# The last pair's row norm ahead of the other pair's transposes at the ends of MLPs and output projections

## The chip, the cores and the metric

The kernel runs on one core of one Trainium2 chip. The metric is the device time of one execution in microseconds (us). Before the change three timed runs gave a median of 3179.25 us (3178.51 to 3179.38). The engines are named as in the profile: PE (TensorE, matmuls and transposes), PEld (its weight loads), DVE (VectorE), ACT (ScalarE), POOL (GpSimd), SP (the queue that issues most DMAs).

## The reference

A forward pass over 512 tokens of 1024 features in fp32, batch 1. The first block has two layers, each a mixer and an MLP with a norm before and after each:

```
for layer in range(DEPTH):
    hn = _rms_norm(x, norm_mix_pre[layer])
    mix = sparse attention + short convolution   # layer 0, ends in @ w_out
          or latent attention                    # layer 1, ends in @ w_o
    x = x + _rms_norm(mix, norm_mix_post[layer])
    hn = _rms_norm(x, norm_ffn_pre[layer])
    x = x + _rms_norm(square(relu(hn @ w1)) @ w2, norm_ffn_post[layer])
```

The second block takes this x with a context of 256 tokens and runs a differential attention and a neighbourhood attention, each on `rms_norm(x) * (1 + scale) + shift` and added back with a gate.

So at the end of each mixer and each MLP of the first block stands the same piece of work: a projection to 1024 columns, an RMS norm of each token's row of the result (the post norm), its addition to x, and an RMS norm of the new row of x (the next norm), whose output feeds the next projection.

## The kernel before

**Products.** An fp32 product is made from three matmuls on halves (`mm3`, L587 to L589): high by high, then the two mixed products of high and low. Every operand therefore exists twice, as hh and hl for activations and as w_hi and w_lo for weights.

**Weights.** `WeightStream` brings weights in units of 128 x 1024 (or 128 x 768). Its `split` takes one unit: ACT casts it to w_hi (L276), POOL subtracts to get w_lo in pieces of two feature blocks (L280), or DVE does this in one instruction where `tick(nc.vector)` is called; then the load of a later unit is issued on SP. `tick` splits the next unit if fewer than `ring` = 4 are ahead of what `release` has given back. So the place of a `tick` in the program sets where cast and subtraction stand in their engines' queues.

**Rows.** The 512 tokens are four tiles of 128 rows, in two pairs. `rows_gemm` (L615) computes such a projection in four column blocks c = 0 to 3 of 256 columns. Blocks 0 and 1 run over all tiles; blocks 2 and 3 go pair by pair, so that pair 0 is complete early. After each tile `evac` squares the result on ACT with a row sum (op_sq), and DVE writes M = result times gain (L1092; in the MLP L1203 and L1206). After a pair's last block comes `tail`: a tick, `post` (L606: sum of squares po_ss, reciprocal root by ACT's rs_y and DVE's rs_a and po_r, then two updates of X, L613), a tick with DVE, and `nx.stat`, the next norm of that pair: squares of X on ACT, reciprocal root, and the scaled rows nf_y on DVE and ACT (L328, L330).

**Transposes.** `Next.flush` turns nf_y into the next stage's operand: for every two feature blocks PE transposes into PSUM (tp, L338), ACT writes hh (L413) and DVE writes hl (L347). Where the next stage has a shift (after MLP 1), DVE writes nf_f (L350), ACT hh, and POOL hl (L416). A pair has eight feature blocks, four such parts. By `PARTS` two parts of pair 0 follow the first tile of pair 1 in block 3 and two follow the second, in front of pair 1's `tail`. Pair 1's own parts are issued by the next stage when it comes to its second half (`need`).

Each engine works off its own queue in program order; a semaphore wait at the head of a queue holds everything behind it. The next stage begins with pair 0's tokens: for an MLP, `first` multiplies four weight units with the 256 columns of pair 0, feature block k = 0 to 7 with three matmuls each, then transposes pair 1 and does the same for its columns.

The places are the ends of the output projection of layer 0 (o0, near 346 us), MLP 0 (near 735), the output projection of layer 1 (o1, near 1010) and MLP 1 (near 1394).

Of the kernel before, what the change touches and what calls it, by code (L numbers as in the profile page):

```python
# [32 lines left out]
def plan():  # L33
# [5 lines left out]
    def mlp(l):  # L39
# [6 lines left out]
        return r  # L46

    p += mlp(0)
    p += [(f"dq:{h}", 2, 384) for h in range(4)]
    p += [(f"dkv:{h}", 3 if h < 2 else 2, 288) for h in range(3)]  # L50
# [6 lines left out]
    p += [(f"v2:7:{h}", 4, 256) for h in range(2)]  # L57
    p += [(f"o1:{c}:{h}", 4, 256) for c in range(4) for h in range(2)]
    p += mlp(1)
    for L in (2, 3):  # L60
        def two(n, g):
# [181 lines left out]
PARTS = ((0, 0), (0, 0), (0, 2), (0, 2))  # L243


class WeightStream:
# [38 lines left out]
    def tick(s, eng=None):  # L285
        if s.halved < min(len(s.units), s.done + s.ring):
            s.split(eng)
# [15 lines left out]
class Next:  # L303
# [55 lines left out]
    def flush(s, n=4):  # L359

        parts = s.pend[0][1]
        for _ in range(min(n, len(parts))):
            parts.pop(0)()
        if not parts:
            s.pend.pop(0)
# [15 lines left out]
class Net:  # L381
# [230 lines left out]
        for j in range(2):  # L612
            nc.vector.scalar_tensor_tensor(s.X[i + j], M[i + j], r[:, j:j + 1], s.X[i + j], OP.mult, OP.add)  # L613

    def rows_gemm(s, keys, lhs, evac, tail, npair, flush, wide_first=False, mid=None, k_first=False):  # L615

        nc = s.nc

        def part(ps, i, u, ks, first, last):
            wh, wl = u  # L620
            t = slice(i * 128, (i + 1) * 128)
            for b, k in enumerate(ks):
                ah, al = lhs(k)
                s.mm3(ps, ah[:, t], al[:, t], wh[:, b], wl[:, b], first and b == 0, last and b == len(ks) - 1)

        def tile(i, c, us, parts=(0, 0)):
            ps = s.mm.tile([128, 512], F32, name="mm")[:, :256]
            for j, (u, ks) in enumerate(us):
                part(ps, i, u, ks, j == 0, j == len(us) - 1)
                if j == 0 and parts[0]:  # L630
                    flush(parts[0])
            s.W.tick()
            evac(i, c, ps)
            if parts[1]:
                flush(parts[1])

        def get(c):
            return [(s.W.get(k), ks) for k, ks in keys(c)]

        def pair(i, c, us, free, between):  # L640

            ps = [s.mm.tile([128, 512], F32, name="mm")[:, :256] for _ in range(2)]
            for j, (u, ks) in enumerate(us):
                for t in range(2):
                    part(ps[t], i + t, u, ks, j == 0, j == len(us) - 1)
                    if free and t:
                        s.W.release(s.W.i - len(us) + 1 + j)
                    s.W.tick()
                    if j == len(us) - 1:
                        evac(i + t, c, ps[t])  # L650
                if j == 0:
                    between()

        n = 2 * npair
        for c in range(2):
            s.W.release()
            us = get(c)
            if c == 0 and wide_first:
                for i0 in range(0, n, 4):
                    ps = [s.mm.tile([128, 512], F32, name="mm")[:, :256] for _ in range(i0, min(n, i0 + 4))]  # L660
                    if k_first:
                        us = [([x[:, b:b + 1] for x in u], [k]) for u, ks in us for b, k in enumerate(ks)]
                    for j, (u, ks) in enumerate(us):
                        for i, q in enumerate(ps):
                            part(q, i0 + i, u, ks, j == 0, j == len(us) - 1)
                    for i, q in enumerate(ps):
                        s.W.tick()
                        evac(i0 + i, c, q)
            elif c == 0:
                for i in range(n):  # L670
                    if mid:
                        mid(i)
                    tile(i, c, us)
            else:
                for i in range(0, n, 2):
                    if mid:
                        mid(4 + i)
                    pair(i, c, us, i == n - 2, lambda: mid and mid(5 + i))
        s.W.release()
        base = s.W.i  # L680
        us = {2: get(2)}
        for p in range(npair):
            for c in (2, 3):
                if c not in us:
                    us[c] = get(c)
                for j in range(2):
                    tile(2 * p + j, c, us[c], PARTS[2 * c + j - 4] if p else (0, 0))
                if p == npair - 1:
                    s.W.release(base + len(us[2]) * (c - 1))
            tail(2 * p, s.W.tick if p == npair - 1 else lambda e=None: None)  # L690
# [390 lines left out]
    def out_proj(s, name, order, lhs, M, ssp, rowt, sqp, make, gain, part=None, late=None):  # L1081

        nc = s.nc

        def evac(i, c, ps):
            cs = slice(c * 256, (c + 1) * 256)
            if part and c == 0:
                nc.vector.tensor_tensor(part[i], part[i], ps, OP.add)
                ps = part[i]
            sq = sqp.tile([128, 256], F32, name="op_sq")  # L1090
            s.act(sq, ps, AF.Square, acc=ssp[:, i, c:c + 1])
            nc.vector.tensor_tensor(M[i][:, cs], ps, rowt[:, cs], OP.mult)  # L1092
            if late and (c, i) == (1, 0):
                late()

        nx = make()

        def tail(i, tick):
            tick()
            s.post(M, ssp, i)  # L1100
            tick(nc.vector)
            nx.stat(s.X[i:i + 2], i, s.p(gain, 0, 8))

        keys = lambda c: [(f"{name}:{c}:{h}", range(4 * h, 4 * h + 4)) for h in (order if c or not part else order[1:])]
        s.rows_gemm(keys, lhs, evac, tail, 2, lambda n: nx.flush(n), wide_first=True, k_first=part is not None)
        return nx

    def mlp(s, l, nx):
        nc, io = s.nc, s.io
        hh, hl = nx.hi, nx.lo  # L1110
        with s.phase():
# [7 lines left out]
            M = [mp.tile([128, D], F32, name=f"M{i}") for i in range(4)]  # L1119
            ssp = mp.tile([128, 4, 4], F32, name="ssp")  # L1120
            g = {}
# [76 lines left out]
            nx = s.after_mlp(l)  # L1198
# [7 lines left out]
                nc.vector.tensor_tensor(M[i][:, cs], t, rowt[:, cs], OP.mult)  # L1206

            def tail(i, tick):
                tick()
                s.post(M, ssp, i)  # L1210
                tick(nc.vector)
                nx.stat(s.X[i:i + 2], i, *nx.gains)
                if l == 0 and i == 0:
                    nx.keep()
                s.keep_x(0 if l else 2, i)

            keys = lambda c: [(f"w2.{l}:3:{c}:{h}", range(4 * h, 4 * h + 4)) for h in range(2)]
            s.rows_gemm(keys, lambda k: g[3, k], evac, tail, 2, lambda n: nx.flush(n), mid=getattr(nx, "mid", None))
        return nx

    def mlp1(s, nx):
# [1169 lines left out]
```

## Time and profile before

| | us |
|---|---|
| median of three timed runs | 3179.25 |
| profiled execution, its own time | 3187.93 |
| its span | 3186.2 |
| PE busy | 3063.2 (96%) |
| DVE busy | 1908.9 (60%) |
| POOL busy | 1742.4 (55%) |
| ACT busy | 1613.7 (51%) |

The profiled execution is one run with the hardware profiler on. In a timeline each row gives start, duration, engine, line, operation, output<-inputs and count; a bracket at the end is the idle time before it on its engine and who ended that. A PE row's duration overlaps the next one's, as matmuls are pipelined. Granted clock 1.00 means TensorE at its upper level.

### The profile page before, as it was taken

To read this page: it belongs to the slowest core of one execution; us is meant where nothing else is said; L and a number is where in the kernel's file an instruction comes from. 1 tells how busy PE (TensorE), PEld (TensorE's weight loads), DVE (VectorE), ACT (ScalarE), POOL (GpSimd) and SP (SyncE) were. 2 spreads that over 40 slices of the span, in tenths; PEclk is the share of its full clock that TensorE was granted. 3 is DMA by queue.
4 is the path that set the end of the run, shared out by engine and by line. 5 is a ranking of instruction groups with operands and counts; after the bars stand their busy time and mean duration, and the time that the engine had idled before them with its cause. 6 is when DMAs were issued, how large, how long until landed. Compare 5 with 4: busy or idle time off the path is not lost.

```text
span 3186.2 us, 59888 instructions
## 1 busy us (share of the span) xinstructions
PE 3063.2 (96%) x22868; PEld 2883.9 (91%) x22868; DVE 1908.9 (60%) x4161; ACT 1613.7 (51%) x3811; POOL 1742.4 (55%) x2398
## 2 busy tenths in 40 slices
PE   8999999998999999998999999998999999999989
PEld 7898889887999988898999999998999999999989
DVE  4875423345774333455777777777445777777764
ACT  4544533345775433344655555555325656555652
POOL 5543466664563666666556655563356455555545
PEclk9999999999999999999999999999999999999989
DMA  3122333434233444422222222213333233333234
GB/s 123 60 74 82 104 126 132 147 115 142 92 95 109 137 142 136 133 94 76 69 70 61 75 69 66 67 61 102 116 105 87 74 88 84 90 90 89 86 96 140
DMA packets 104555, 310.89 MB, mean 98 GB/s; under 512 B 19902, under 2 KB 33470, under 8 KB 100684
## 3 DMA queue, kind: packets, MB, share of 16 engines
q1 hardware_dynamic: 94908, 271.60, 26.4%
q0 software_dynamic: 7776, 31.46, 4.3%
q10 hardware_dynamic: 1584, 4.00, 0.4%
q8 instruction: 181, 2.97, 0.4%
q14 instruction: 106, 0.87, 0.1%
HBM read 258.73 MB, written 23.12 MB: 88 GB/s over the span
## 4 chain that ended last, share of the span: by engine, by line
PE 62%; DVE 4%; ACT 3%; DMA 3%; POOL 2%; issue 1%; SPq 0%; DVEq 0%; ACTq 0%; POOLq 0%
PE mm L587 16%; PE mm L589 15%; PE mm L588 15%; PE mm L2165 3%; DMA KL<-KL 2%; PE s L2105 2%; PE tp L2304 2%; PE tp L2152 1%; PE s L2106 1%; POOL w_lo L280 1%; PE mm L2319 1%; PE mm L2314 1%; ACT X L413 1%; PE s L2278 1%; PE tp L1843 1%
## 5 line engine op out<-in xcount | busy, mean ns | idle before, releaser
L280 POOL TENSOR_TENSOR w_lo<-w_raw,w_hi 128x256 fp32r<-128x256 f32 (+2 forms) x1446 | 1145.7, 825 | 816.2 <-ACT w_hi L276 786.3
L587 PE MATMUL mm<-w_hi,hh 128*128 128x256 f32 (+2 forms) x2752 | 803.0, 292 | 11.6 <-ACT w_hi L276 4.4
L588 PE MATMUL mm<-w_lo,hh 128*128 128x256 f32 (+2 forms) x2752 | 784.7, 285 | 5.4 <-POOL w_lo L280 3.9
L589 PE MATMUL mm<-w_hi,hl 128*128 128x256 f32 (+2 forms) x2752 | 783.8, 285 | 1.1 <-POOL hl L416 1.1
L587 PEld LDWEIGHTS mm<-w_hi,hh 128*128 128x128 f32 x2752 | 525.8, 191 | 22.1 <-ACT df_sq L413 8.5
L588 PEld LDWEIGHTS mm<-w_lo,hh 128*128 128x128 f32 x2752 | 526.5, 191 | 14.2 <-POOL w_lo L280 8.9
L589 PEld LDWEIGHTS mm<-w_hi,hl 128*128 128x128 f32 x2752 | 525.0, 191 | 2.5 <-POOL hl L416 1.8
L276 ACT CAST w_hi<-w_raw 128x1024 fp32r<-128x1024 f32 (+2 forms) x371 | 383.0, 1036 | 210.5 <-PE mm L589 171.1
L587 PE MATMUL mm<-hh,w_hi 128*128 128x256 f32 (+1 forms) x1408 | 455.5, 324 | 3.0 <-DVE M L1092 2.9
L588 PE MATMUL mm<-hl,w_hi 128*128 128x256 f32 (+1 forms) x1408 | 449.0, 319 | 0.6
L589 PE MATMUL mm<-hh,w_lo 128*128 128x256 f32 (+1 forms) x1408 | 447.6, 318 | 0.6 <-DVE w_lo L280 0.6
L587 PEld LDWEIGHTS mm<-hh,w_hi 128*128 128x128 f32 x1408 | 266.8, 190 | 30.8 <-issue 5.2
L587 PE MATMUL mm<-w_hi,gh 128*128 128x256 f32 x1024 | 287.8, 281 | 0.0
L589 PE MATMUL mm<-w_hi,gl 128*128 128x256 f32 x1024 | 287.1, 280 | 0.1
L588 PEld LDWEIGHTS mm<-hl,w_hi 128*128 128x128 f32 x1408 | 266.9, 190 | 22.3 <-DVE hl L347 1.7
L588 PE MATMUL mm<-w_lo,gh 128*128 128x256 f32 x1024 | 287.0, 280 | 0.0
L589 PEld LDWEIGHTS mm<-hh,w_lo 128*128 128x128 f32 x1408 | 266.5, 189 | 21.4 <-DVE w_lo L280 1.0
L416 DVE TENSOR_TENSOR gl<-rsq,gh 128x512 fp32r<-128x512 f32 x64 | 46.2, 721 | 268.7 <-ACT gh L413 268.7
L587 PEld LDWEIGHTS mm<-w_hi,gh 128*128 128x128 f32 x1024 | 193.2, 189 | 0.4
L589 PEld LDWEIGHTS mm<-w_hi,gl 128*128 128x128 f32 x1024 | 193.0, 188 | 0.5 <-DVE gl L416 0.5
L588 PEld LDWEIGHTS mm<-w_lo,gh 128*128 128x128 f32 x1024 | 193.0, 188 | 0.3
L1831 POOL TENSOR_TENSOR SZ<-SZ,ge 128x128 f32<-128x128 f32 x154 | 80.3, 523 | 162.2 <-DVE ge L1829 68.9
(385 smaller groups left out, 6948.8 us busy)
## 6 DMA issues: line engine op xcount, KB each, us to landing
w_raw<-in_w SPq DMA_DIRECT2D x352, 512.0 KB, 3.6
modw<-in_mod SPq DMA_DIRECT2D x24, 1024.0 KB, 5.7
KH<-KH POOLq DMA_DIRECT2D x32, 384.0 KB, 3.5
KL<-KL POOLq DMA_DIRECT2D x32, 384.0 KB, 4.9
xs<-X SPq DMA_DIRECT2D x12, 512.0 KB, 3.6
X<-xs SPq DMA_DIRECT2D x12, 512.0 KB, 8.4
yd<-ob SPq DMA_DIRECT2D x16, 384.0 KB, 2.5
w_raw<-in_w SPq DMA_DIRECT2D x8, 552.0 KB, 3.6
```

The costliest lines, as they stand in the source:

```text
L276: nc.scalar.copy(hi[:, :m], raw[:, :m])
L280: (eng or nc.gpsimd).tensor_tensor(lo[:, c], raw[:, c], hi.bitcast(F32)[:, c], OP.subtract)
L413: return s.nc.scalar.activation(out, in_, func, bias=bias, scale=scale, **kw)
L416: (eng or s.nc.vector).tensor_tensor(lo, x, hi.bitcast(F32), OP.subtract)
L587: mm(ps, ah, bh, start=first, stop=False)
L588: mm(ps, ah, bl, start=False, stop=False)
L589: mm(ps, al, bh, start=False, stop=last)
L1831: nc.gpsimd.tensor_tensor(z, z, x, OP.mult)
L1843: nc.tensor.transpose(pt[:, j], rawt[n][:, i, pr * 128:(pr + 1) * 128], s.ident)
L2105: nc.tensor.matmul(o, q, KH[:, h, a:b], start=True, stop=False)
L2165: nc.tensor.matmul(ps, x["w"][:, k], V[g][:, kb, p * 128:(p + 1) * 128], start=k == 0, stop=k == nk - 1)
L2304: nc.tensor.transpose(t[:, k], x["P"][:, k * 128:(k + 1) * 128], s.ident)
```

## The change

`rows_gemm` gets a flag `early_post`, set by `out_proj` and `mlp`. With it, a tick stands ahead of the first tile of the last pair's block 3, and the last tile issues no transposes. `tail` now does `post` first, then (for the last pair) the two parts of transposes that the last tile left, then two ticks, both with POOL, then `nx.stat`.

```
-    def rows_gemm(s, keys, lhs, evac, tail, npair, flush, wide_first=False, mid=None, k_first=False):
+    def rows_gemm(s, keys, lhs, evac, tail, npair, flush, wide_first=False, mid=None, k_first=False, early_post=False):
...
                 for j in range(2):
-                    tile(2 * p + j, c, us[c], PARTS[2 * c + j - 4] if p else (0, 0))
+                    last = p == npair - 1 and c == 3 and early_post
+                    if last and j == 0:
+                        s.W.tick()
+                    tile(2 * p + j, c, us[c], (0, 0) if not p or last and j else PARTS[2 * c + j - 4])
...
         def tail(i, tick):
+            s.post(M, ssp, i)
+            if i:
+                nx.flush(2)
             tick()
-            s.post(M, ssp, i)
-            tick(nc.vector)
+            tick()
             nx.stat(s.X[i:i + 2], i, s.p(gain, 0, 8))
```

The tail of `mlp` is changed in the same way. PE's order and SP's do not change. On DVE at the end of o0, where M_3774 and M_3775 are the last two tiles and X_68 and X_69 their rows, the order before is:

```order
L1092 TENSOR_TENSOR M_3775<-mm,rowt 128x256
L347 SCALAR_TENSOR_TENSOR hl<-tp,par,hh 128x256 x4
L609 TENSOR_REDUCE po_ss<-ssp 128x2
L422 TENSOR_SCALAR rs_v<-po_ss 128x2
L432 TENSOR_TENSOR rs_a<-rs_y 128x2
L433 SCALAR_TENSOR_TENSOR rs_a<-rs_a,rs_v 128x2
L434 SCALAR_TENSOR_TENSOR po_r<-rs_a,rs_y 128x2
L613 SCALAR_TENSOR_TENSOR X_68<-M_3774,po_r,X_68 128x1024
L613 SCALAR_TENSOR_TENSOR X_69<-M_3775,po_r,X_69 128x1024
L280 TENSOR_TENSOR w_lo<-w_raw,w_hi 128x1024
L422 TENSOR_SCALAR rs_v<-nf_ss 128x2
```

and now, at the same place:

```order
L1095 TENSOR_TENSOR M_3775<-mm,rowt 128x256
L609 TENSOR_REDUCE po_ss<-ssp 128x2
L422 TENSOR_SCALAR rs_v<-po_ss 128x2
L432 TENSOR_TENSOR rs_a<-rs_y 128x2
L433 SCALAR_TENSOR_TENSOR rs_a<-rs_a,rs_v 128x2
L434 SCALAR_TENSOR_TENSOR po_r<-rs_a,rs_y 128x2
L613 SCALAR_TENSOR_TENSOR X_68<-M_3774,po_r,X_68 128x1024
L613 SCALAR_TENSOR_TENSOR X_69<-M_3775,po_r,X_69 128x1024
L347 SCALAR_TENSOR_TENSOR hl<-tp,par,hh 128x256 x4
L422 TENSOR_SCALAR rs_v<-nf_ss 128x2
```

The four hl of pair 0 (feature blocks 4 to 7) went from in front of the row norm to behind it, and the w_lo of DVE is gone (POOL has it). On ACT at the same place the order before is:

```order
L276 CAST w_hi<-w_raw 128x1024
L413 ACTIVATE op_sq,ssp<-mm 128x256
L413 ACTIVATE hh<-tp,par 128x256 x4
L276 CAST w_hi<-w_raw 128x1024
L413 ACTIVATE op_sq,ssp<-mm 128x256
L413 ACTIVATE hh<-tp,par 128x256 x4
L276 CAST w_hi<-w_raw 128x1024
L413 ACTIVATE rs_y<-po_ss,eps 128x2
L413 ACTIVATE rs_y<-rs_y 128x2
L276 CAST w_hi<-w_raw 128x1024
L413 ACTIVATE nf_y,nf_ss<-X_68 128x1024
```

and now:

```order
L276 CAST w_hi<-w_raw 128x1024 x2
L413 ACTIVATE op_sq,ssp<-mm 128x256
L413 ACTIVATE hh<-tp,par 128x256 x4
L413 ACTIVATE op_sq,ssp<-mm 128x256
L413 ACTIVATE rs_y<-po_ss,eps 128x2
L413 ACTIVATE rs_y<-rs_y 128x2
L413 ACTIVATE hh<-tp,par 128x256 x4
L276 CAST w_hi<-w_raw 128x1024 x2
L413 ACTIVATE nf_y,nf_ss<-X_68 128x1024
```

The second unit's cast moved ahead of the first hh block; the third and fourth moved behind the second hh block. At MLP 1, where POOL also writes hl, POOL's order before is:

```order
L280 TENSOR_TENSOR w_lo<-w_raw,w_hi 128x256 x28
L416 TENSOR_TENSOR hl<-nf_f,hh 128x256 x4
L280 TENSOR_TENSOR w_lo<-w_raw,w_hi 128x256 x4
L416 TENSOR_TENSOR hl<-nf_f,hh 128x256 x4
L280 TENSOR_TENSOR w_lo<-w_raw,w_hi 128x256 x4
```

and now:

```order
L280 TENSOR_TENSOR w_lo<-w_raw,w_hi 128x256 x32
L416 TENSOR_TENSOR hl<-nf_f,hh 128x256 x8
L280 TENSOR_TENSOR w_lo<-w_raw,w_hi 128x256 x8
```

The four w_lo of the second unit stand ahead of all hl, and eight w_lo (those of the third unit, and of the fourth, which DVE did) behind them.

## Rows read from the trace of the kernel before

**Rows 1.** The page: busy us (share of span) and instructions by engine.
```profile
PE 3063.2 (96%) x22868; PEld 2883.9 (91%) x22868; DVE 1908.9 (60%) x4161; ACT 1613.7 (51%) x3811; POOL 1742.4 (55%) x2398
```

**Rows 2.** Timeline of PE, end of o0: start, us, ..., [idle before <-releaser].
```profile
346.58 0.39 PE L587 MATMUL mm<-hh,w_hi 128*128 128x256 f32 x1 [1.40 <-DVE M L1092]
...
349.45 0.39 PE L588 MATMUL mm<-hl,w_hi 128*128 128x256 f32 x1
...
356.20 0.39 PE L589 MATMUL mm<-hh,w_lo 128*128 128x256 f32 x1 [0.33 <-DVE w_lo L280]
...
358.88 1.48 PE L338 MATMUL tp<-ident,nf_y 128*128 128x128 f32 x12
361.69 0.63 PE L338 MATMUL tp<-ident,nf_y 128*128 128x128 f32 x4 [1.33 <-DVE hl L347]
```

**Rows 3.** Timeline of DVE, end of o0, norm of pair 1.
```profile
346.10 0.42 DVE L1092 TENSOR_TENSOR M<-mm,rowt 128x256 f32<-128x256 f32 x1 [0.82 <-ACT op_sq L413]
346.47 0.48 DVE L347 SCALAR_TENSOR_TENSOR hl<-tp,par,hh 128x256 fp32r<-128x256 f32 x1
...
348.91 0.48 DVE L347 SCALAR_TENSOR_TENSOR hl<-tp,par,hh 128x256 fp32r<-128x256 f32 x1 [0.54 <-ACT hh L413]
349.31 0.15 DVE L609 TENSOR_REDUCE po_ss<-ssp 128x2 f32<-128x8 f32 x1
...
350.69 0.66 DVE L433 SCALAR_TENSOR_TENSOR rs_a<-rs_a,rs_v 128x2 f32<-128x2 f32 x1
...
352.15 2.86 DVE L613 SCALAR_TENSOR_TENSOR X<-M,po_r,X 128x1024 f32<-128x1024 f32 x2
```

**Rows 4.** Timeline of DVE, o0, norm of pair 0.
```profile
333.00 0.15 DVE L609 TENSOR_REDUCE po_ss<-ssp 128x2 f32<-128x8 f32 x1
...
334.34 2.48 DVE L613 SCALAR_TENSOR_TENSOR X<-M,po_r,X 128x1024 f32<-128x1024 f32 x2
```

**Rows 5.** Timeline of POOL, end of o0.
```profile
341.65 2.83 POOL L280 TENSOR_TENSOR w_lo<-w_raw,w_hi 128x256 fp32r<-128x256 f32 x4 [16.85 <-ACT w_hi L276]
```

**Rows 6.** Timeline of ACT, end of o0.
```profile
353.84 1.07 ACT L413 ACTIVATE nf_y<-X 128x1024 f32<-128x1024 f32 x1 [2.66 <-DVE X L613]
```

**Rows 7.** Timeline of DVE, end of o1.
```profile
1015.50 2.85 DVE L613 SCALAR_TENSOR_TENSOR X<-M,po_r,X 128x1024 f32<-128x1024 f32 x2
```

**Rows 8.** Timeline of PE, end of MLP 0.
```profile
737.33 0.44 PE L587 MATMUL mm<-w_hi,hh 128*128 128x384 f32 x1 [0.49 <-ACT w_hi L276]
...
742.98 0.69 PE L588 MATMUL mm<-w_lo,hh 128*128 128x384 f32 x1 [0.78 <-DVE w_lo L280]
745.33 1.27 PE L338 MATMUL tp<-ident,nf_y 128*128 128x128 f32 x4 [0.38 <-DVE nf_y L328]
```

**Rows 9.** Timeline of ACT, end of MLP 0.
```profile
740.89 1.06 ACT L413 ACTIVATE nf_y<-X 128x1024 f32<-128x1024 f32 x1 [2.46 <-DVE X L613]
```

**Rows 10.** Windows of PE: stretch, us, PE busy (x), granted clock, DMA share, GB/s.
```profile
740.00:743.00 3.00, 2.22 (x8) 0.50 0.51 147
743.00:747.00 4.00, 3.62 (x12) 0.53 0.77 262
1390.00:1395.00 5.00, 2.43 (x19) 1.00 0.34 105
1395.00:1399.00 4.00, 4.00 (x19) 0.57 0.20 44
```

**Rows 11.** Timeline of PE, end of MLP 1.
```profile
1394.05 0.39 PE L587 MATMUL mm<-w_hi,hh 128*128 128x256 f32 x1 [2.01 <-ACT w_hi L276]
...
1408.61 0.39 PE L587 MATMUL mm<-w_hi,hh 128*128 128x256 f32 x1 [1.81 <-ACT sq L413]
```

**Rows 12.** Timeline of DVE, end of MLP 1.
```profile
1392.07 0.54 DVE L350 TENSOR_SCALAR nf_f<-tp,ada,adb 128x256 f32<-128x256 f32 x1 [2.52 <-POOL hl L416]
...
1401.94 2.92 DVE L613 SCALAR_TENSOR_TENSOR X<-M,po_r,X 128x1024 f32<-128x1024 f32 x2
```

**Rows 13.** Timeline of ACT, end of MLP 1.
```profile
1403.70 1.06 ACT L413 ACTIVATE nf_y<-X 128x1024 f32<-128x1024 f32 x1 [2.65 <-DVE X L613]
```

More of the change, by code (lines that the diff above doesn't have):

```diff
@@ L1098, in tail @@
         def tail(i, tick):
+            s.post(M, ssp, i)
+            if i:
+                nx.flush(2)
             tick()
-            s.post(M, ssp, i)
-            tick(nc.vector)
+            tick()
             nx.stat(s.X[i:i + 2], i, s.p(gain, 0, 8))
         keys = lambda c: [(f"{name}:{c}:{h}", range(4 * h, 4 * h + 4)) for h in (order if c or not part else order[1:])]
-        s.rows_gemm(keys, lhs, evac, tail, 2, lambda n: nx.flush(n), wide_first=True, k_first=part is not None)
+        s.rows_gemm(keys, lhs, evac, tail, 2, lambda n: nx.flush(n), wide_first=True, k_first=part is not None, early_post=True)
         return nx
@@ L1208, in tail @@
             def tail(i, tick):
+                s.post(M, ssp, i)
+                if i:
+                    nx.flush(2)
                 tick()
-                s.post(M, ssp, i)
-                tick(nc.vector)
+                tick()
                 nx.stat(s.X[i:i + 2], i, *nx.gains)
@@ L1217, in mlp @@
             keys = lambda c: [(f"w2.{l}:3:{c}:{h}", range(4 * h, 4 * h + 4)) for h in range(2)]
-            s.rows_gemm(keys, lambda k: g[3, k], evac, tail, 2, lambda n: nx.flush(n), mid=getattr(nx, "mid", None))
+            s.rows_gemm(keys, lambda k: g[3, k], evac, tail, 2, lambda n: nx.flush(n), mid=getattr(nx, "mid", None), early_post=True)
         return nx
```

## The prediction, as it was made before the result was known

> **What bounds the kernel now.** I read the busy times of the page first: TensorE (PE) is busy for 96% of the span, the next engine, DVE, for 60% [rows 1]. So a change pays only where PE stands still, and costs wherever it makes PE stand. Then I read the PE timeline at the four places that the diff touches, looking for brackets (idle time and who ended it), and at each bracket the timeline of the releaser. The reader is to see there which of three streams PE waits for at the end of a stage: the weights of the next stage (w_hi by ACT, w_lo by POOL or DVE), the transposed activations of the first pair (hh by ACT, hl by DVE or POOL), or the second pair's norm (X, then nf_y).
>
> At the end of the first output projection PE waits 1.40 us for the last M at 346.58, then runs into the next MLP's first half; its matmul at 349.45 starts just as the last hl of the first pair is ready (348.91 + 0.48 = 349.39) [rows 2, 3]. PE follows the hl block on DVE there, and the row norm with its X updates comes after that block, at 349.31, where PE needs nothing of it: the pair-1 transposes at 358.88 start without a bracket [rows 2]. That is the heart of this case: of the two streams on DVE the early one is what PE wants next.
>
> **The change part by part.** Four places: the ends of o0, MLP 0, o1, MLP 1. The order of PE and of SP's DMA issues is the same in both kernels; only ACT, DVE and POOL change.
>
> (1) *The row norm ahead of the second four hl of pair 0, at o0 and o1.* Start of the norm: M at 346.10 stays where it is. It waits for an op_sq that stands on ACT behind a cast and four hh before, and behind four hh with the cast ahead of them now; the sum is the same. So po_ss starts at about 346.5, in the place of the first hl (346.47). In front of the hl block now stands everything from po_ss to the end of the second X. This stretch is in the trace twice: for pair 0, with POOL idle, 333.00 to 334.34 + 2.48, which is 3.82 us [rows 4]; for pair 1, 349.31 to 352.15 + 2.86, which is 5.70 us [rows 3]. The long one ran beside w_lo on POOL. In the new order POOL subtracts the first unit from 341.65, 2.83 us for four pieces [rows 5], and the second right after, until about 347.3; the norm from 346.5 overlaps by some 0.8 us and then has POOL idle. I take 4.2, near the short row; 3.8 and 5.7 are the ends. PE does k = 0 to 3 as before, three matmuls each, then stands until the first of the four hl, and follows the rest in the old step. So the whole block, and PE behind it, is 4.2 late.
>
> The rows show why the ends lie apart: the two X updates take 2.48 us in the one and 2.86 in the other, and in the long one a two-column operation like rs_a takes 0.66 [rows 3, 4]. The Trainium skill ("SBUF — State Buffer", section "🔬 SBUF: two separate sides") says that the port pair shared by VectorE and GpSimd is an exclusive lock, and that a VectorE operation with two SBUF inputs blocks against a GpSimd operation that reads SBUF. By that rule the 5.70 holds only where POOL is at work, and the choice of 4.2 agrees with it; did the rule not hold, the sum would go by 5.70 at both sites, 3.0 us more.
>
> (2) *The vector w_lo goes to POOL, at o0 and o1.* PE waits 0.33 for it at 356.20 [rows 2]; that bracket goes: -0.3. POOL has the piece ready later than DVE would, but PE also arrives some 4 us later. The casts of units 3 and 4 now stand behind the hh chain on ACT, about 4 us later than before; with 2.83 for each unit's four w_lo [rows 5] the fourth unit's first piece is there at about 357.6, and PE comes to it at 356.20 - 0.33 + 3.9 = 359.8. Hidden by PE's first-half matmuls; without that cover it costs up to about 2 us.
>
> (3) *nf_y of pair 1 at o0 and o1.* X is done earlier (350.7 against 355.0), but the squares on ACT, at 353.84 before [rows 6], now stand behind the hh chain and two casts, at about 355. nf_y is ready near 360; PE arrives at 358.88 + 3.9. Nothing. The flush itself, 1.33 of waiting for hl at 361.69 [rows 2], is unchanged.
>
> Net of (1) to (3): 4.2 - 0.3 = 3.9 at o0, and at o1, where the same rows recur (X at 1015.50 took 2.85 [rows 7]), again 3.9: +7.8. Bounds per site 3.2 and 5.7.
>
> (4) *Clock.* A PE that stands some 4 us may be granted less afterwards. Rows: over 1390 to 1395 PE was busy 2.43 of 5 us, and the next 4 us have a granted clock of 0.57, near the lower of its levels (1.2 of 2.4 GHz) [rows 10]. By how much one stall of 4 us does this no row says. Half a clock over 1.6 us on average costs 0.8: +0.8 a site, ends 0 and 3.4, +1.6 for two.
>
> (5) *MLP 0.* PE waits 0.49 at 737.33 for the third unit's w_hi [rows 8]. That cast stands behind the four hh in both kernels, and these now wait for the norm: about +4.1, so PE resumes at about 741.4. What bounds the end of this stage is the second pair's nf_y: the transposes at 745.33 wait 0.38 for it [rows 8]. Its squares began at 740.89, 2.46 after ACT fell idle [rows 9]; now the hh chain and two casts (0.82 each) stand ahead, until about 742.2: +1.3. On the other side w_lo waits go (the vector one of 0.78 [rows 8] among them). PE arrives at the transposes between 746.6 (nf_y) and about 748, since 740 to 743 was already at a clock of 0.50 before [rows 10]. I take +2.3, from 0.5 to 5.
>
> (6) *MLP 1* (the shift version: nf_f on DVE, hh on ACT, hl on POOL). The second unit's cast no longer stands behind the hh, so the wait of 2.01 at 1394.05 goes [rows 11]. Yet PE is stopped later anyway: at 1408.61 it waits 1.81 for evacuations on ACT that stand behind nf_y [rows 11], whose squares started at 1403.70 [rows 13]. So the 2.01 counts only if nf_y is not later. The second unit's four w_lo (2.83) now precede hl on POOL, so the fourth nf_f, which waited 2.52 for a buffer until 1392.07 [rows 12], moves to about 1394.9, and po_ss to 1396.5 where it was 1398.2. Add 3.82 to 5.70: X ends at 1400.3 to 1402.2, against 1401.94 + 2.92 before [rows 12]. Then nf_f, hl and hh of the second half, about 2.9, until 1403.1 to 1405, and two casts, 2.0: squares at 1405.1 or later, +1.4. PE also lacks hl of k = 4 to 7 until about 1403, which puts its own work some 2 us late. I take +2.0, from -1 to +4.
>
> **Sum.** 7.8 + 1.6 + 2.3 + 2.0 = 13.7 us, against a profiled execution of 3187.93 (span 3186.2, 1.7 around it). The three timed runs have a median of 3179.25, 8.7 lower; I carry the difference over: 3193.0, +0.43%.
>
> **The rivals.**
> *The clock decides.* After the weak stretch in MLP 0 PE ran 740 to 747 near the lower level [rows 10]. If each new stall at o0, o1 and MLP 0 brings such a 6.8 us stretch, each costs 3.4 more: 7.8 + 10.2 + 2.3 + 2.0 = 22, less the 1.6 not double-counted: about 3200. For it speaks the row 1395 to 1399 at 0.57 after a poor stretch [rows 10]; against it that k = 0 to 3 run right before the new stall. The Trainium skill ("TensorE: Matmul & The Clock Gate", section "HAM oscillation — how this bites in real kernels") describes matmul loops whose waits put the clock back each time, which would give this case. Chance 0.14.
>
> *Given back.* PE's lateness is absorbed by waits that it has anyway: 1.40 + 0.33 + 1.33 at each projection [rows 2]. They would have to be waits for something that does not move with hl; only the 0.33 is. If also X's run were fast (3.2 a site) and MLP 0 and 1 came out at zero or below, the sum is 6.4 - 3, about +3: 3182.5, not distinguishable. Chance 0.13.
>
> *Faster.* The units formed sooner decide. In MLP 1 the 2.01 goes together with the half-clock stretch behind it, 4 us at 0.57, some 1.7 us [rows 10, 11]; in MLP 0 the brackets of 0.49, 0.78 and 0.38 [rows 8] and the slow 6.8 us, 3.4; 0.33 at each projection: about 9, so 3170. This needs one thing: that the norm is through before PE comes to k = 4: from 346.58 to 349.45 it starts 22 matmuls, 0.13 each, so twelve take it to 348.1 [rows 2]. With a start at 346.5 it would have to take 1.5 us, and the two X alone take 2.48 [rows 4]. Chance 0.06.
>
> *The change does not do what it says.* Only the first two units are formed sooner; the third and fourth come some 4 us later at every place. If these are what PE then waits for, step (2) costs its 2 us at each projection: about 3197, inside the range. Chance 0.03.
>
> **How the numbers follow.** Forecast 3193.0 with 0.64, its own range 3186 to 3199. Slower by over 0.2% (6.4 us, about what separates a change from none here): 0.64 + 0.14 + 0.03 = 0.81. Within: 0.13. Faster: 0.06. Upper end: the ends 5.7 twice, 5 and 4 with half the clock term give +22; lower end: 3.2 twice, 0.5, -1, no clock, +5.9, and part of the given-back case: 3182.5 to 3203.
>
> **What the new profile would show.** At the end of o0 and o1: po_ss at about 346.5 (in this profile's time), X within 4 us after, and the four hl only then; a new PE bracket of some 3 to 4 us on an L588 matmul, released by hl of DVE; no bracket for w_lo of DVE. In MLP 0 a wait for w_hi several times 0.49. In MLP 1 no wait at 1394 for w_hi, but one for hl of POOL some us long. I am wrong if PE has no new bracket of over 2 us behind the projections, if M's op_sq came much earlier, or if the clock columns after these brackets fall to half for longer than 2 us.

## The result, and the profile after

The change made the kernel slower. The first six runs of each gave a median of 3198.90 us (3195.68 to 3200.29) against 3180.14 before (3178.51 to 3185.89); the ratio of the means is 1.0053, with a 95% interval of 1.0040 to 1.0066, that is 13 to 21 us. The prediction said 3193.0, between 3182.5 and 3203, with 0.81 for slower. Later runs of the kernel before, made beside the experiments, have medians of 3184.36, 3183.04 and 3183.62 (21, 21 and 10 runs), so the first six were on its low side.

The two profiled executions take 3200.19 and 3187.93, 12.3 apart. Both kernels issue the same 22868 PE instructions in the same order, so the n-th start in one can be held against the n-th in the other. This difference is called lateness; what it gains from ahead of a place to behind it is what the place cost. Places by the time of the kernel before: o0 from 340 to 400, MLP 0 from 726 to 800, o1 from 1000 to 1040, MLP 1 from 1380 to 1440. In the changed kernel: +4.92, -0.33, +4.81, +2.80, together 12.2. The rest of the span cancels in these two executions: +1.4 before 340 and +1.6 near 694 stand at stretches of the clock's lower level (0.66 over 50 to 55 and 0.57 over 700 to 704 in the changed kernel) that some other kernels of the study lack, and -3.0 in small steps after 1440, whose causes were not traced, offset them. So 12.2 is what the places show, and its nearness to 12.3 is in part chance.

The busy times answer to [rows 1]. PE's rose by 3.9 of the 12.2 us, 3063.2 to 3067.1; the rest is idle time.

```profile
PE 3067.1 (96%) x22868; PEld 2887.8 (90%) x22868; DVE 1902.9 (59%) x4157; ACT 1611.4 (50%) x3811; POOL 1748.9 (55%) x2412
```

The end of o0 on PE, answering to [rows 2]; this execution is 1.43 us late there already.

```profile
348.01 0.39 PE L587 MATMUL mm<-hh,w_hi 128*128 128x256 f32 x1 [1.03 <-DVE M L1095]
...
352.21 0.58 PE L588 MATMUL mm<-hl,w_hi 128*128 128x256 f32 x1 [2.37 <-DVE hl L347]
...
354.69 0.55 PE L588 MATMUL mm<-hl,w_hi 128*128 128x256 f32 x1
...
365.25 1.48 PE L338 MATMUL tp<-ident,nf_y 128*128 128x128 f32 x12
368.05 0.63 PE L338 MATMUL tp<-ident,nf_y 128*128 128x128 f32 x4 [1.33 <-DVE hl L347]
```

The new bracket of 2.37 stands at k = 4, the fifth product's second matmul, and its releaser is the first of the four hl. The row at 354.69 is the same matmul at k = 7, the one that reads the last hl. The bracket on the vector w_lo is absent, and nf_y still has none. DVE over the same stretch, answering to [rows 3]:

```profile
347.54 0.41 DVE L1095 TENSOR_TENSOR M<-mm,rowt 128x256 f32<-128x256 f32 x1
347.88 0.15 DVE L609 TENSOR_REDUCE po_ss<-ssp 128x2 f32<-128x8 f32 x1
...
349.28 2.48 DVE L613 SCALAR_TENSOR_TENSOR X<-M,po_r,X 128x1024 f32<-128x1024 f32 x2
351.68 0.48 DVE L347 SCALAR_TENSOR_TENSOR hl<-tp,par,hh 128x256 fp32r<-128x256 f32 x1
...
358.65 0.66 DVE L432 TENSOR_TENSOR rs_a<-rs_y 128x2 f32<-128x2 f32 x1
```

POOL beside it:

```profile
343.06 5.57 POOL L280 TENSOR_TENSOR w_lo<-w_raw,w_hi 128x256 fp32r<-128x256 f32 x8 [16.86 <-ACT w_hi L276]
```

From po_ss to the first hl it is 3.80 us, the short form of [rows 4]: POOL's two units ran from 343.06 to 348.63, and X began behind that. Then the windows of PE around the stall: stretch, its length, busy, granted clock, DMA share, GB/s.

```profile
348.00:351.00 3.00, 1.83 (x13) 1.00 0.59 187
351.00:354.00 3.00, 1.79 (x6) 0.64 0.14 55
354.00:357.00 3.00, 3.00 (x16) 0.50 0.01 3
357.00:360.00 3.00, 3.00 (x21) 0.72 0.32 91
360.00:364.00 4.00, 4.00 (x37) 1.00 0.71 232
```

The clock is at its lower level (1.2 GHz, 0.50) for over 6 us behind the stall: 3 us hold 16 matmuls at 0.50, and 4 us hold 37 at 1.00. The end of o1 has the same bracket, and a shorter stretch at the lower level, which begins some 2 us after PE resumed:

```profile
1021.84 0.38 PE L588 MATMUL mm<-hl,w_hi 128*128 128x256 f32 x1 [2.40 <-DVE hl L347]
```
```profile
1021.00:1024.00 3.00, 2.02 (x9) 1.00 0.02 8
1024.00:1027.00 3.00, 2.87 (x13) 0.55 0.00 0
1027.00:1030.00 3.00, 3.00 (x24) 0.88 0.47 128
```

Lateness, matmul by matmul, parts the wait from the clock. At the matmul that reads the last hl PE is 3.82 us later than at the start of the stage (o0; 3.79 at o1), as the hl block is. From there, with nothing more to wait for, it grows by 1.75 (1.52) while the clock is low, and where the wait for the vector w_lo had been it falls by 0.6.

At the end of MLP 0 the wait for the third unit's w_hi, 0.49 in [rows 8], is 4.34, and the transposes behind it wait for nothing:

```profile
749.17 0.69 PE L587 MATMUL mm<-w_hi,hh 128*128 128x384 f32 x1 [4.34 <-ACT w_hi L276]
750.26 0.69 PE L588 MATMUL mm<-w_lo,hh 128*128 128x384 f32 x1 [0.40 <-POOL w_lo L280]
755.32 0.60 PE L338 MATMUL tp<-ident,nf_y 128*128 128x128 f32 x4
```

At the end of MLP 1 the wait for w_hi of [rows 11] is gone; a wait for hh and the old hold by evacuations are there:

```profile
1413.63 0.58 PE L587 MATMUL mm<-w_hi,hh 128*128 128x256 f32 x1 [2.26 <-ACT hh L413]
1423.37 0.39 PE L587 MATMUL mm<-w_hi,hh 128*128 128x256 f32 x1 [1.99 <-ACT sq L413]
```

and on DVE, answering to [rows 12], the fourth nf_f waits twice as long for its buffer, because POOL has eight w_lo ahead of hl now:

```profile
1407.29 0.54 DVE L350 TENSOR_SCALAR nf_f<-tp,ada,adb 128x256 f32<-128x256 f32 x1 [5.26 <-POOL hl L416]
...
1410.19 2.48 DVE L613 SCALAR_TENSOR_TENSOR X<-M,po_r,X 128x1024 f32<-128x1024 f32 x2
```

### The profile page after: what moved, and what is told of

The parts are those of the page before. It is cut to its first block, busy times and chain, and to the rows that moved or that the text cites. A ratio compares the mean times of both kernels' runs of the same rounds, so it can differ in the third digit from the quotient of the medians.

```text
span 3198.4 us, 59896 instructions
## 1 busy us (share of the span) xinstructions
PE 3067.1 (96%) x22868; PEld 2887.8 (90%) x22868; DVE 1902.9 (59%) x4157; ACT 1611.4 (50%) x3811; POOL 1748.9 (55%) x2412
## 4 chain that ended last, share of the span: by engine, by line
PE 59%; DVE 4%; POOL 4%; ACT 3%; DMA 3%; issue 3%; SPq 0%; POOLq 0%; ACTq 0%; DVEq 0%
PE mm L587 15%; PE mm L589 14%; PE mm L588 14%; PE mm L2172 3%; POOL w_lo L280 2%; DMA KL<-KL 2%; PE s L2112 2%; PE tp L2311 1%; PE tp L2159 1%; PE s L2113 1%; PE mm L2326 1%; ACT X L413 1%; PE mm L2321 1%; PE s L2285 1%; PE tp L1850 1%
## 5 line engine op out<-in xcount | busy, mean ns | idle before, releaser
L280 POOL TENSOR_TENSOR w_lo<-w_raw,w_hi 128x256 fp32r<-128x256 f32 (+1 forms) x1460 | 1153.4, 822 | 824.5 <-ACT w_hi L276 809.3
```

What stands on the lines that cost most here:

```text
L280: (eng or nc.gpsimd).tensor_tensor(lo[:, c], raw[:, c], hi.bitcast(F32)[:, c], OP.subtract)
```

## The experiments

The table holds lateness gained over each place, from the profiled execution of each kernel against that of the kernel before, and the timed ratio with its interval. "filled" kernels have extra matmuls, which are left out of the count.

| kernel | o0 | MLP 0 | o1 | MLP 1 | sum, us | ratio to before (95%) |
|---|---|---|---|---|---|---|
| the change | +4.92 | -0.33 | +4.81 | +2.80 | +12.2 | 1.0053 (1.0040 to 1.0066) |
| only_projections | +4.72 | -0.05 | +4.64 | -0.20 | +9.1 | 1.0035 (1.0022 to 1.0047) |
| only_mlps | -0.01 | -0.58 | +0.05 | +2.98 | +2.4 | 1.0011 (1.0002 to 1.0019) |
| ticks_only | +0.70 | -0.55 | +0.70 | +2.34 | +3.2 | 1.0008 (0.9999 to 1.0017) |
| move_only | +6.03 | +0.21 | +5.02 | +3.12 | +14.4 | 1.0051 (1.0039 to 1.0064) |
| norm_split | +0.58 | -1.95 | +0.65 | +5.31 | +4.6 | 1.0024 (1.0015 to 1.0033) |
| stall_filled | +9.64 | -0.40 | +8.90 | +5.82 | +24.0 | 1.0071 (1.0057 to 1.0085) |
| stall_filled_2 | +3.19 | -0.28 | +3.30 | +3.44 | +9.7 | 1.0029 (1.0017 to 1.0042) |
| mlp1_four_buffers | -0.01 | -0.47 | +0.07 | -1.05 | -1.5 | 0.9998 (0.9989 to 1.0007) |

A ratio of 1.001 is 3.2 us. The sums lie inside the intervals or within about half a microsecond of them. Lateness is of one profiled execution of each kernel.

**Where: the projections alone, the MLPs alone.** only_projections takes `early_post` and the new tail out of `mlp`:

```
-            s.rows_gemm(keys, lambda k: g[3, k], evac, tail, 2, ..., early_post=True)
+            s.rows_gemm(keys, lambda k: g[3, k], evac, tail, 2, ...)
```

> The change at the two output projections alone, both MLP ends as before. Theory (PE is held by the four hl that now stand behind the row norm): a PE bracket of about 2.4 us released by hl of DVE at each of the two places and 4.9 us of lateness gained over each, so 9.5 to 13 us slower than before, most of the whole change. Rival 1 (the cost sits in the MLP ends, where the third and fourth weight unit come later and PE waits 4.3 us for w_hi): under 4 us. Rival 2 (the weights formed sooner pay, but only at the MLPs): no more here than the theory says, but the whole change would then be cheaper than this part.

only_mlps takes them out of `out_proj` in the same way.

> The change at the two MLP ends alone, both projections as before. Theory: in MLP 0 a wait of about 4 us for w_hi that is given back by the next stage's waits (0 to +2 in all), in MLP 1 +2 us: together 2 to 5 us slower. Rival 1: 10 us or more. Rival 2 (what it gains is hidden by the lateness from the projections): faster than before by 1 to 3 us.

Each part costs in its own places what it costs in the whole: 9.4 us at the two projections, some three quarters of the loss, and 2.4 at the MLPs. Rival 1 of both falls, and the parts add up (9.1 + 2.4 against 12.2), so the one does not hide the other.

**What: the ticks or the move.** ticks_only keeps the new ticks and puts the transposes back in front of the norm:

```
-                    tile(2 * p + j, c, us[c], (0, 0) if not p or last and j else PARTS[2 * c + j - 4])
+                    tile(2 * p + j, c, us[c], PARTS[2 * c + j - 4] if p else (0, 0))
...
             s.post(M, ssp, i)
-            if i:
-                nx.flush(2)
             tick()
             tick()
```

> At all four places the new ticks (second unit sooner, third and fourth after the norm with w_lo on POOL), but the second four hl stay in front of the row norm. Theory: the PE bracket on hl behind the projections is gone, the wait for the vector w_lo (0.33 at each projection) too; MLP 0 within 1.5 of before; MLP 1 up to 2 later, since the second unit's w_lo stand ahead of hl on POOL: within 3 us of before. Rival 1 (the later third and fourth units are the cost): 8 us slower or more.

move_only does the opposite:

```
-                    if last and j == 0:
-                        s.W.tick()
...
             tick()
-            tick()
+            tick(nc.vector)
```

> At all four places the row norm ahead of the second four hl, but the ticks as before the change (no early tick, the last w_lo on DVE behind the hl). Theory: 4.9 us or a little more at each projection, since the w_lo on DVE now comes later still, and 2 to 5 at the MLPs: 12 to 20 us slower than before. Rival 1 (units): under 5 us slower.

The move is the cost at the projections: 6.0 and 5.0 by itself, against 0.7 each for the ticks. PE in the move_only kernel at the end of o0:

```profile
350.28 0.58 PE L588 MATMUL mm<-hl,w_hi 128*128 128x256 f32 x1 [3.41 <-DVE hl L347]
```

The bracket is 3.41 where the full change has 2.37, 1.04 more, and DVE shows why: po_ss to the first hl takes 4.84 us there (344.91 to 349.75) instead of 3.80, since POOL's second unit, cast later without the early tick, runs from 344.24 to 347.03, beside the norm's small operations.

```profile
344.24 2.79 POOL L280 TENSOR_TENSOR w_lo<-w_raw,w_hi 128x256 fp32r<-128x256 f32 x4 [1.30 <-ACT w_hi L276]
345.66 0.70 DVE L432 TENSOR_TENSOR rs_a<-rs_y 128x2 f32<-128x2 f32 x1
346.40 0.66 DVE L433 SCALAR_TENSOR_TENSOR rs_a<-rs_a,rs_v 128x2 f32<-128x2 f32 x1
347.09 0.16 DVE L434 SCALAR_TENSOR_TENSOR po_r<-rs_a,rs_y 128x2 f32<-128x2 f32 x1
```

The third, behind POOL's end, takes 0.16. At o1 the bracket is 3.45 and the lateness at the last hl the same 4.84 as at o0; that o1 cost 1.0 less is the clock, 0.8 there against 1.8 at o0.

ticks_only did not go quite as expected at the projections. The wait for the fourth unit's w_lo went (-0.6), but PE now waits for the third unit's (lateness +0.8) and again late in the first half (+0.4), both POOL's. POOL's eight pieces took 7.84 us there, beside the X updates, where they take 5.57 without them.

```profile
346.18 0.39 PE L587 MATMUL mm<-hh,w_hi 128*128 128x256 f32 x1 [1.03 <-DVE M L1095]
353.90 0.39 PE L589 MATMUL mm<-hh,w_lo 128*128 128x256 f32 x1 [0.58 <-POOL w_lo L280]
```
```profile
350.62 7.84 POOL L280 TENSOR_TENSOR w_lo<-w_raw,w_hi 128x256 fp32r<-128x256 f32 x8 [3.83 <-ACT w_hi L276]
```

At MLP 1 the ticks alone cost 2.34 and the move alone 3.12, where the whole change costs 2.80: either suffices, and they do not add. With the ticks the second unit's w_lo stand in front of POOL's hl, and the fourth nf_f waits 5.28; with the move alone it waits 2.50, as before, and the later nf_f stand behind the norm.

**How much of the norm: small operations or X.** norm_split is the changed kernel with the hl between the norm's small operations and X:

```
         s.rstd(r, ss, 1.0 / D)
+        if mid:
+            mid()                     # nx.flush(2) for the last pair
         for j in range(2):
             nc.vector.scalar_tensor_tensor(s.X[i + j], ...)
```

> The changed kernel, but the second four hl stand between the norm's small operations (po_ss to po_r) and the two X updates. In the changed kernel's profile the small ones take 1.40 us (347.88 to 349.28) and the X updates 2.40 (to 351.68). Theory (PE is late by what stands ahead of the hl on DVE): the PE bracket on hl shrinks to nothing or a few tenths, the hl block comes 1.4 later than before the change instead of 3.8, each projection costs 1 to 1.5 us instead of 4.9; MLP ends about as in the kernel with the new ticks alone (-0.6 and +2). In all 2 to 5 us slower than before. Rival (X, and with it nf_y of pair 1, is what PE misses behind a projection): each projection still costs 3 us or more.

At the projections the theory holds: 0.58 and 0.65 instead of 4.9, less than the expected 1 to 1.5, since PE got back 0.6 of it where the wait for w_lo had been. No clock is lost there either. DVE shows the hl 1.22 us behind po_ss:

```profile
344.43 0.15 DVE L609 TENSOR_REDUCE po_ss<-ssp 128x2 f32<-128x8 f32 x1
...
345.65 0.47 DVE L347 SCALAR_TENSOR_TENSOR hl<-tp,par,hh 128x256 fp32r<-128x256 f32 x1
```

That X begins 2.7 us later behind po_ss there (4.06 instead of 1.40) harms nothing, so the rival falls. Of this study's kernels with the move, this one costs least at the projections. At MLP 1 the kernel lost 5.3 instead of 2. There PE resumed earlier than before and ran into POOL's hl of pair 1, 2.20 us, and into the clock's lower level behind it (0.53 over 1424.29 to 1427.00, 0.50 over 1427.00 to 1430.41):

```profile
1424.29 0.45 PE L589 MATMUL mm<-w_hi,hl 128*128 128x256 f32 x1 [2.20 <-POOL hl L416]
```

POOL began its own work of that stage only at 1407.50, right behind its last w_lo. That this stage is held by POOL's queue, as these rows suggest, was not foreseen; no run tested it.

**Is the clock a price of the stall?** stall_filled and stall_filled_2 put 27 matmuls into PE's order at the place of the stall, in `first`, for the first block of the first half:

```
+ for ks, n in ((range(4), 18), (range(4, 5), 3), (range(5, 6), 3), (range(6, 7), 3), (range(7, 8), 0)):
+     s.fmm(pss[b][:, c], [us[b]], hh, hl, 0, 256, ks=ks)
+     for _ in range(n):
+         nc.tensor.matmul(OUT, us[0][0][:, 0, :128], hh[:, 0, :256], start=True, stop=True)
```

where OUT is `fill[:, :256]`, a tile of the tp pool, in the first, and `pss[3][:, 256:512]` in the second.

> The changed kernel with 27 extra matmuls of 256 columns in the first half of each MLP's first stage, 18 between k = 3 and k = 4 and three each behind k = 4, 5 and 6, written to a transposition buffer that nobody reads: work for PE in the time in which it waits for hl. If the clock's fall behind the stall (0.64, 0.50, 0.72 over 351 to 360) is a cost of the stall, it goes, and each projection costs 3.3 us instead of 4.9, although PE has 27 more matmuls: 3 us faster than the changed kernel. Rival (the slow rows after the stall are the hl chain, not the clock): no change or up to 1 us slower per place.

This one told nothing of the clock: the tile itself waited for the last hl, so the matmuls came after the stall, on top of it.

```profile
351.61 4.18 PE L1169 MATMUL tp<-hh,w_hi 128*128 128x256 f32 x18 [5.04 <-DVE hl L347]
```

> As stall_filled, but the extra matmuls write to PSUM columns of the MLP's own last accumulator that are started anew later, so that they wait for nothing but PE's order. (In stall_filled they went to a transposition buffer and waited 5.04 us until the last hl had given it back, so they stood behind the stall and not in it.) If the clock's fall is a price of the stall, the granted clock over the 8 us behind it stays at 1.00 and each projection costs 3.3 us instead of 4.9, with 27 more matmuls. Rival (no clock term, the 1.6 us are the hl chain): each projection costs 4.9 or more.

Here they run where they should, and the clock stays up:

```profile
347.77 2.32 PE L1168 MATMUL mm<-hh,w_hi 128*128 128x256 f32 x18
...
350.44 0.39 PE L588 MATMUL mm<-hl,w_hi 128*128 128x256 f32 x1 [0.22 <-DVE hl L347]
```
```profile
349.00:352.00 3.00, 2.73 (x21) 1.00 0.15 61
352.00:355.00 3.00, 3.00 (x28) 1.00 0.01 3
355.00:358.00 3.00, 3.00 (x28) 1.00 0.29 79
```

With 27 useless matmuls more at each projection PE is 1.73 and 1.51 us less late (4.92 to 3.19, 4.81 to 3.30). The price without the clock is thus 3.2 to 3.3, and the clock behind it costs another 1.5 to 1.7, as the lateness of the changed kernel had it. The timed ratios point the same way, 1.0029 (1.0017 to 1.0042) against 1.0053 (1.0040 to 1.0066).

**Can the end of MLP 1 be made faster than before?** mlp1_four_buffers changes the kernel before:

```
-        nx.open("2b")
+        nx.open("2b", 3, 4)           # four nf_f buffers
...
-            s.W.tick()
+            s.W.tick(eng)             # nc.vector for the last tile of MLP 1
```

> The kernel before, changed at the end of MLP 1 alone: four instead of three nf_f buffers, and the w_lo of the second unit (the last tile's tick) on DVE. Theory (at MLP 1 the fourth nf_f waits 2.52 and 2.71 us for a buffer that POOL's hl gives back, with hh, the cast, po_ss and nf_y behind it): the PE wait of 2.01 for w_hi falls to under 1, nf_y and the hold at 1408.61 come 2 to 3 us sooner, in all 2 to 3 us faster than before over that place. Rival (POOL's hl or ACT is what the end of MLP 1 waits for in any order): within 0.5 us of before.

PE's wait of 2.01 for w_hi is gone, one of 0.99 for the w_lo of DVE stands in its place, and the hold by evacuations ends 1.96 earlier. By 1440 only 1.05 is left: the hold is longer now, and over the 6.6 us behind it the clock stood at 0.59 (1407.73 to 1414.30), where the kernel before had 0.74 (1408.61 to 1415.20).

```profile
1394.23 0.38 PE L588 MATMUL mm<-w_lo,hh 128*128 128x256 f32 x1 [0.99 <-DVE w_lo L280]
1407.73 0.58 PE L587 MATMUL mm<-w_hi,hh 128*128 128x256 f32 x1 [3.44 <-ACT sq L413]
```

The gain of 1.05 is half of the lower end that was expected, and the timed ratio cannot tell the kernel from the one before. No version of this study is shown to be faster than the kernel before.

## Why the prediction was right

**The core, step (1), held.** The long form of the norm belongs to a busy POOL: in the three DVE rows of move_only, two operations take 0.70 and 0.66 beside POOL's subtractions, and the one behind POOL's end takes 0.16. By the Trainium skill ("SBUF — State Buffer", section "🔬 SBUF: two separate sides"), the rule that the prediction weighed, the port pair of VectorE and GpSimd is an exclusive lock for which a VectorE operation with two SBUF inputs and a GpSimd operation that reads SBUF contend; these rows agree. PE is held by the four hl that now stand behind the norm, at both projections. The stretch ahead of them measured 3.80 us where 4.2 was taken; 3.8 was the lower end, so the bracket is 2.37 where 3 to 4 had been forecast. (The bounds of 3.2 and 5.7 a site do not follow from the terms, which give 3.5 and 5.4.) The kernels with the move have the bracket on hl and those without it do not, and norm_split moves the cost with the length of what stands ahead.

**Steps (2) and (3) held.** The waits for w_lo are gone. Lateness fell by 0.6 there (6.98 at 355, 6.37 at 357); 0.3 had been taken. nf_y of pair 1 stayed hidden, though some 0.5 later than thought: its small operations took 0.66 each beside POOL (the last DVE row of o0 above), it was ready at 361.9, and PE came at 365.25.

**Step (4), the clock, was too small by half.** It took 0.8 a site; 1.5 to 1.7 is what stall_filled_2 shows. The prediction had named clock columns at half for longer than 2 us as a sign of being wrong, and this sign came: on the clock it was wrong. The errors of (1), (2) and (4) nearly cancel, 4.7 a projection predicted, 4.92 and 4.81 measured; that this sum fits so closely is luck. The rival of 3.4 more a site is refuted in size, right in kind. (Its time of about 3200 takes off 1.6 that its sum does not hold.) At o0 its long stretch came, but for the first 2.5 us of it (352.21 to 354.69) PE was following the hl block anyway, so only the rest cost time.

**Step (5), MLP 0, had the wrong sum.** The wait for w_hi came as forecast (4.34; lateness was 7.90 ahead of the place and 11.84 there, so PE resumed 3.9 later, where 4.1 had been estimated), and at the transposes PE was 2.1 late, the predicted 2.3. What failed is that this was taken to last. The kernel before ran these transposes at the lower level, the changed one at the upper, and that gave back 0.8 by 748; and the kernel before has a second such stretch at 767, behind a wait of 2.38 (2.31 in the changed kernel). In the kernel before it reads

```profile
767.00:770.00 3.00, 2.79 (x12) 0.54 0.55 180
```

and in the changed one

```profile
776.00:779.00 3.00, 2.64 (x20) 1.00 0.60 180
```

The stretch is there in all three profiles with the old end of MLP 0 (0.53 to 0.55 over the 3 us behind the wait in before, only_projections and mlp1_four_buffers) and missing in all seven with a changed one (1.00). So it goes with the end of MLP 0; why the same wait lowers the clock in the one and not in the other stays open. Net: -0.33 instead of +2.3.

**Step (6), MLP 1, had the right size,** +2.8 against +2.0, with the order of causes as given: POOL's w_lo ahead of hl, a later norm, later nf_y. That these are the causes is read from the rows and not shown apart: ticks_only costs 2.34 there and move_only 3.12. The forecast wait for POOL's hl came as one of 2.26 for ACT's hh. X ended at 1410.19 + 2.48 = 1412.7, which less the 12.5 of lateness on entry is 1400.2, beside a forecast of 1400.3 to 1402.2.

**The sum.** 13.7 predicted; 12.2 by places, 12.3 between the profiled executions, 13 to 21 by the first timed runs. The errors of the places, +0.2, -2.6, +0.1 and +0.8, add up to -1.5. The absolute time came out 5.9 above the forecast; nearly 5 of this is that the forecast was hung on three runs of the kernel before with a median of 3179.25, where its later runs lie near 3184. "Given back" fits the outcome of one place of four, MLP 0, and there the clock gave back a good part of it, which that rival had not named.

## What to carry to other kernels

Before moving work ahead of other work on an in-order engine, find which of the two the bottleneck engine needs first, and by how much: here PE needed hl within 1.7 us of the stage's start and the row norm's result only 12 us later. A wait of 2.4 us on a full PE, with the chain behind it, cost 3.2 to 3.3 us by itself and 1.5 to 1.7 us more by the clock, and one of 3.4 us cost 0.8 at one place and 1.8 at the other by the clock. So a stall is priced with the granted clock of the windows behind it, and the price can be tested by filling the stall with idle work. Compare two executions by the n-th instruction of the bottleneck engine, place by place: differences of 0.5 us show there, where the whole time varies by 5.

## What was not expected of the hardware

The small two-column operations on DVE take 0.16 us alone and 0.66 us beside POOL's subtractions (rs_a at 340.21 and at 358.65 to 359.34 in the changed kernel), and a pair of X updates 2.48 alone and up to 3.45 beside them (ticks_only at 1402.01). POOL is slowed too: eight pieces that take 5.57 alone took 7.62 beside the X updates of norm_split (at 349.07) and 7.84 in ticks_only. And matmuls that compute nothing made the changed kernel faster, though not as fast as the kernel before: with them the clock behind the stall stayed at 1.00 instead of 0.50.
